# Hymba-style decoder block with PEER experts: both parts of the split weights kept in DRAM, and the raw U blocks moved to a pool of their own

## The chip, the cores and the metric

One core of a Trainium2 chip runs the whole layer in one launch. The metric is the device time of that core in microseconds (us), lower is better. The five compute engines are named as in the profile: PE (TensorE, with PEld for its weight loads), DVE (VectorE), ACT (ScalarE), POOL (GpSimd) and SP (SyncE, which here only issues DMAs).

## The reference

1024 tokens of width 1024 pass through one layer. What matters here is where the weight matrices are used:

```python
ada = jax.nn.silu(c) @ w_ada + b_ada          # shift, scale, gate of both norms
h = modulate(rms_norm(x, norm1_g), shift1, scale1)
proj = h @ w_in + b_in                        # q | k | v | B | C | u_conv, 2304 columns
mix = concat(head-normed attention, head-normed short gated conv) @ w_out + b_out
x = x + gate1 * mix
h2 = modulate(rms_norm(x, norm2_g), shift2, scale2)
q = h2 @ w_query                              # 8 heads x 256, 2048 columns
# PEER: top 16 of 16 x 16 pairs of keys per head, softmax gates,
#   a = gelu(h2 . peer_u[idx]);  y = sum(gate * a * peer_v[idx]),  16384 experts
x = x + gate2 * peer(h2, q);  return rms_norm(x, final_g)
```

## The kernel before

The tokens are eight tiles of 128. The **front** (everything up to the gates of PEER) runs in three groups: group 0 holds tiles 0, 1, 2, group 1 tiles 3, 4, 5 (both 384 tokens wide), group 2 tiles 6 and 7 (256 wide). After the front comes the **dense part**: for tiles 0, 1, 3, 4, 5 all 16384 experts are evaluated in blocks of 128 (U, then gelu, then the gates, then V), while for tiles 2, 6, 7 POOL gathers only the chosen rows of U and V by indirect DMA. The gathers and the making of the dense gates are spread beside the front and the dense part.

Every float32 matrix product is made of three matmuls in the rounded type fp32r. An operand X is split into H, X rounded, and L = X - H, and the product is H·h_H + H·h_L + L·h_H. `lin` (line 279) does this for one block of 128 output columns: 24 matmuls, for each of two halves of the rows first the eight that need H, then the four that need L.

The weights of the front are 42 such blocks in each group: 18 of w_in, 8 of w_out, 16 of w_query. One block is 512 KB of float32. The class `Weights` hands them out. `take()` gives the next block and calls `load()` for the one behind it, so that one block is prepared ahead of the one in use. `load()` does this:

- line 223: SP fetches the raw block into one of two buffers (tag `wraw`), in every group
- line 230: ACT makes H of each half (a copy with rounding), in every group
- line 232, group 0 only: POOL makes L of each half; line 225 writes L to a DRAM tile `low` at the next call, behind the next raw fetch
- line 235, groups 1 and 2: L comes back from `low` with a DMA of 256 KB a half

H and L have four buffers each (tags `wH`, `wL`), which is two blocks. In DRAM the rounded copy H is never kept, so ACT makes it anew in each group.

Other users of the same resources: `wada` (line 750), 48 blocks of 512 KB of w_ada, are fetched by SP in group 0 and reduced on DVE (`adaacc`, lines 754 and 756); the first 24 are needed before the first norm. `keyg` (line 631) brings the keys of a head in the query stage. In groups 1 and 2 the dense gates are made: `oh` (lines 834 to 847) on DVE, ACT and POOL, `G` (line 857) on PE, a copy to `stg` on ACT (line 858) and a DMA `G_d<-stg` (line 860) that ACT issues, 2 MB each in pieces of 256 bytes, 20 in all. The dense part begins with the fetch of two raw U blocks, the gates `Gb` and three V blocks; ACT makes UH (line 1096), POOL UL (line 1100), and PE starts with `A` (line 1133).

In the front a scheduler, which simulates the engines as the program is built, sets the order of the instructions of each engine; the dense part follows an order written out in the code. DMAs of SP and ACT take their completion semaphores in turn from a set of eight, and one that takes a semaphore waits until the DMA eight places before it has landed.

Of the kernel before, what the change touches and what calls it, by code (L numbers as in the profile page):

```python
# [9 lines left out]
F32 = mybir.dt.float32  # L10
F32R = mybir.dt.float32r
# [7 lines left out]
P = 128  # L19
# [3 lines left out]
NC = D // P  # L23
# [61 lines left out]
def block_kernel(  # L85
# [18 lines left out]
    nc = tc.nc  # L104
# [45 lines left out]
    gp = ctx.enter_context(tc.tile_pool(name="gp", bufs=ROWS[0]))  # L150
    gs = ctx.enter_context(tc.tile_pool(name="gs", bufs=1))
    slx = ExitStack()
    with ExitStack() as fctx:
# [48 lines left out]
        class Weights:  # L202


            def __init__(self):
                self.src = [(w_in, k) for k in range(18)] + [(w_out, k) for k in range(NC)]
                self.src += [(w_query, k) for k in range(16)]
                self.n = len(self.src)
                self.src *= len(GROUPS)
                self.at, self.ready = 0, []  # L210

                self.low = [dr.tile([P, 2, NC // 2, P], F32, name=f"low{k}") for k in range(self.n)]
                self.keep = []

            def load(self):
                if self.at == len(self.src):
                    return
                dram, k = self.src[self.at]
                name = f"{self.at}"
                low, first = self.low[self.at % self.n], self.at < self.n  # L220
                self.at += 1
                raw = fs.tile([P, NC, P], F32, tag="wraw", name=f"raw_{name}", bufs=2)
                nc.sync.dma_start(raw.rearrange("p c j -> p (c j)"), dram[k])
                while self.keep:
                    nc.sync.dma_start(*self.keep.pop(0))
                for q in range(2):
                    src = raw[:, q * (NC // 2) : (q + 1) * (NC // 2), :]
                    H = fs.tile([P, NC // 2, P], F32R, tag="wH", name=f"H_{name}_{q}", bufs=4)
                    L = fs.tile([P, NC // 2, P], F32R, tag="wL", name=f"L_{name}_{q}", bufs=4)
                    nc.scalar.copy(H, src)  # L230
                    if first:
                        nc.gpsimd.tensor_tensor(L, src, H.bitcast(F32), op=ALU.subtract)
                        self.keep.append((low[:, q], L.bitcast(F32)))
                    else:
                        nc.sync.dma_start(L.bitcast(F32), low[:, q])
                    self.ready.append((H, L))

# [774 lines left out]

        with tc.tile_pool(name="f0", bufs=1) as f0:
            rest = [lambda n=n: ada_rest(f0, n) for n in range(4, 12)]
            fronts[0].fp = f0
# [33 lines left out]
        gates_of = Beside(dense_gates(gg, [3, 4, 5]))  # L1049
        with tc.tile_pool(name="f2", bufs=1, reuse_waits="tile") as f2:  # L1050
            last.hH = f2.tile([P, NC, 2 * P], F32R, name="hSH")
            last.hL = f2.tile([P, NC, 2 * P], F32R, name="hSL")
# [20 lines left out]
    def dense_experts():  # L1073

        Up = {}
        Ur = {}
        Vr = {}
# [4 lines left out]
        def load_G(j):  # L1082

            if j < NK // GB:
                Gt[j] = dp.tile([P, NTG, GB * TG], F32, tag="G", name=f"Gb{j}", bufs=2)
                nc.sync.dma_start(Gt[j], G_d[j])

        def fetch_U(b):
            raw = dp.tile([P, NC, P], F32, tag="U", name=f"U{b}", bufs=2)
            nc.sync.dma_start(raw.rearrange("p c j -> p (c j)"), peer_uT[b])  # L1090
            Ur[b] = raw

# [112 lines left out]
        def load_ends():  # L1205

            gather.rest()
            for name, src in (("g2", g2_d[0]), ("fg", final_g)):
                r = dp.tile([P, NC, P], F32, tag="U", name=name, bufs=2).rearrange("p c j -> p (c j)")
                nc.sync.dma_start(r, src.partition_broadcast(P))  # L1210
                shared.append(r)
# [33 lines left out]

        fetch_U(0)
        fetch_U(1)
        for j in range(2):
# [160 lines left out]
```

## Time and profile before

| | |
|---|---|
| median of 3 runs | 2824.21 us (2823.27 to 2829.01) |
| profiled execution | 2822.61 us, span 2820.8 us, mean granted clock 0.974 |
| busy in the span | PE 2642.3 us (94%), DVE 2165.8 (77%), POOL 1696.2 (60%), ACT 1033.5 (37%) |
| group 0 of the front | 0 to 326 us, of which 0 to 46 before the first `lin` |
| group 1, group 2 | 326 to 664 us, 664 to 981 us |
| dense part | 981 to 2820 us |

The span is that of the engines' instructions; the execution's own time is 1.8 us longer, for what lies around them. The rows below come from the same execution. A row of busy times by stretch tells how full each engine and the DMA rings were there; the chain of waits tells which work ended last at each moment, and only what stands on that chain can shorten the run directly. The granted clock is TensorE's, 1.00 being 2.4 GHz.

### The profile page before, as it was taken

What the parts mean: (1) busy time and instruction counts of PE and PEld (TensorE: products, weight loads), DVE (VectorE), ACT (ScalarE), POOL (GpSimd) and SP (SyncE); (2) the same over time, 40 slices, a digit from 0 to 9 for tenths busy, and PEclk for the clock granted to TensorE, in tenths of its full rate; (3) what the DMA queues carried; (4) which work ended last, traced back from release to release, by engine and by line L of the source; (5) the groups of instructions that cost most, each with busy time, mean ns of one, the idle gap of its engine ahead of it and who ended that gap; (6) DMA issues with size and microseconds to landing.
All of it is one profiled execution on the core that took longest, in us unless ns stands there. A gap on an engine that the chain in (4) does not pass through costs nothing.

```text
span 2820.8 us, 44152 instructions
## 1 busy us (share of the span) xinstructions
PE 2642.3 (94%) x15358; PEld 2405.9 (85%) x15358; DVE 2165.8 (77%) x4645; ACT 1033.5 (37%) x2219; POOL 1696.2 (60%) x1726
## 2 busy tenths in 40 slices
PE   5998989988898869999999999999999999999997
PEld 4788977888788869999999899999998899999996
DVE  8835996879786877787777777777877777777776
ACT  3345555664667432222222222222222322222222
POOL 2334533523333247778777677777776777777771
PEclk9999999999999989999999999999999999999999
DMA  9757669986689949898889898989888888889884
GB/s 345 285 182 245 210 201 290 277 290 210 171 224 263 293 132 342 311 339 327 327 321 332 286 350 315 341 310 338 321 325 324 331 325 327 326 324 334 313 326 145
DMA packets 418268, 816.70 MB, mean 290 GB/s; under 512 B 192630, under 2 KB 198774, under 8 KB 418044
## 3 DMA queue, kind: packets, MB, share of 16 engines
q0 software_dynamic: 110592, 402.70, 38.8%
q1 hardware_dynamic: 143292, 369.24, 37.2%
q10 hardware_dynamic: 164160, 41.94, 6.9%
q8 instruction: 120, 1.97, 0.3%
q14 instruction: 104, 0.85, 0.1%
HBM read 739.83 MB, written 73.94 MB: 288 GB/s over the span
## 4 chain that ended last, share of the span: by engine, by line
PE 72%; DVE 13%; DMA 5%; issue 4%; ACT 3%; POOL 2%; SPq 0%; ACTq 0%; DVEq 0%; POOLq 0%
PE A L1133 29%; PE V L1179 29%; PE G L857 3%; PE lin_g1in L279 2%; DVE oh L834 2%; DVE adaacc L756 2%; DMA G_d<-stg 1%; PE lin_g0o L279 1%; DMA wada<-in_w_ada_dram 1%; PE lin_g2in L279 1%; PE po L430 1%; DVE Skg L143 1%; DVE ti L145 1%; PE lin_g2o L279 1%; DVE ti L142 1%
## 5 line engine op out<-in xcount | busy, mean ns | idle before, releaser
L960 POOL DMA_INDIRECT u<-in_peer_u_dram,idx x384 | 365.8, 952 | 264.5 <-DVE u L981 126.7
L1179 PE MATMUL V<-VH,WH 128*128 128x512 f32 x1280 | 501.4, 392 | 12.9 <-DVE acc_d L1186 10.3
L988 DVE SCALAR_TENSOR_TENSOR acc<-v,wv,acc 128x1024 f32<-128x1024 f32 x381 | 489.4, 1285 | 15.1 <-DMA v<-in_peer_v_dram,idx 10.9
L1179 PE MATMUL V<-VL,WH 128*128 128x512 f32 x1280 | 500.1, 391 | 0.0
L1179 PE MATMUL V<-VH,WL 128*128 128x512 f32 x1280 | 499.3, 390 | 0.0
L960 POOL DMA_INDIRECT v<-in_peer_v_dram,idx x384 | 363.5, 947 | 210.7 <-DVE u L981 69.1
L981 DVE SCALAR_TENSOR_TENSOR u<-u,h 128x1024 f32<-128x1024 f32 x384 | 457.7, 1214 | 5.8 <-DMA u<-in_peer_u_dram,idx 5.8
L1138 ACT ACTIVATE A<-A 128x384 f32<-128x384 f32 (+1 forms) x256 | 107.7, 422 | 955.7 <-PE A L1133 940.9
L1133 PE MATMUL A<-hDH,UH 128*128 128x384 f32 (+1 forms) x2048 | 345.5, 311 | 18.7 <-ACT UH L1096 18.1
L1116 POOL TENSOR_TENSOR VL<-V,VH 128x512 fp32r<-128x512 f32 x256 | 332.0, 1310 | 34.9 <-ACT VH L1112 32.6
L1133 PE MATMUL A<-hDH,UL 128*128 128x384 f32 (+1 forms) x2048 | 343.3, 310 | 8.5 <-POOL UL L1100 8.5
L1133 PEld LDWEIGHTS A<-hDH,UH 128*128 128x128 f32 x2048 | 321.9, 190 | 29.5 <-ACT UH L1096 18.9
L1133 PE MATMUL A<-hDL,UH 128*128 128x384 f32 (+1 forms) x2048 | 342.9, 310 | 0.0
L1100 POOL TENSOR_TENSOR UL<-U,UH 128x1024 fp32r<-128x1024 f32 x128 | 308.8, 2413 | 31.9 <-ACT UH L1096 29.7
L1133 PEld LDWEIGHTS A<-hDH,UL 128*128 128x128 f32 x2048 | 311.8, 189 | 9.8 <-POOL UL L1100 9.8
L1150 DVE TENSOR_TENSOR A<-A,Gb 128x384 f32<-128x384 f32 (+1 forms) x256 | 126.2, 498 | 248.3 <-ACT A L1138 243.6
L1133 PEld LDWEIGHTS A<-hDL,UH 128*128 128x128 f32 x2048 | 312.6, 190 | 0.0
L1179 PEld LDWEIGHTS V<-VH,WH 128*128 128x128 f32 x1280 | 241.3, 188 | 60.7 <-DVE acc_d L1186 12.0
L847 POOL TENSOR_TENSOR oh<-oh,gT 128x512 f32<-128x512 f32 x120 | 131.3, 1095 | 261.8 <-DVE oh L834 207.5
L1179 PEld LDWEIGHTS V<-VH,WL 128*128 128x128 f32 x1280 | 241.3, 188 | 51.4
L1179 PEld LDWEIGHTS V<-VL,WH 128*128 128x128 f32 x1280 | 241.3, 189 | 45.3
L1186 DVE TENSOR_TENSOR acc_d<-acc_d,V 128x512 f32<-128x512 f32 x310 | 211.7, 683 | 84.9 <-PE V L1179 84.8
(313 smaller groups left out, 4190.8 us busy)
## 6 DMA issues: line engine op xcount, KB each, us to landing
U<-in_peer_uT_dram SPq DMA_DIRECT2D x128, 512.0 KB, 7.7
V<-in_peer_v_dram SPq DMA_DIRECT2D x256, 256.0 KB, 3.8
L<-low SPq DMA_DIRECT2D x168, 256.0 KB, 4.0
G_d<-stg ACTq DMA_DIRECT2D x20, 2048.0 KB, 16.7
Gb<-G_d SPq DMA_DIRECT2D x64, 640.0 KB, 7.4
raw<-in_w_in_dram SPq DMA_DIRECT2D x54, 512.0 KB, 4.7
wada<-in_w_ada_dram SPq DMA_DIRECT2D x48, 512.0 KB, 6.8
raw<-in_w_query_dram SPq DMA_DIRECT2D x48, 512.0 KB, 5.2
```

Of the source, the lines that this page charges most:

```text
L279: nc.tensor.matmul(ps[:, :w], wt[:, c, :], h[:, q * (NC // 2) + c, o : o + w], start=(k == 0), stop=(k == 3 * NC - 1),)
L847: nc.gpsimd.tensor_tensor(og, og, gT[:, t0 : t0 + 4].unsqueeze(2).to_broadcast([P, 4, NK]), op=ALU.mult)
L960: nc.gpsimd.indirect_dma_start(out=t, out_offset=None, in_=peer_u if which == "u" else peer_v, in_offset=bass.IndirectOffsetOnAxis(ap=idx[ ...
L981: nc.vector.scalar_tensor_tensor(t, t, 1.0, h2[i], op0=ALU.mult, op1=ALU.mult, accum_out=av[i][:, j : j + 1])
L988: nc.vector.scalar_tensor_tensor(acc[i], t, wv[i][:, j : j + 1], acc[i], op0=ALU.mult, op1=ALU.add)
L1100: nc.gpsimd.tensor_tensor(L, Ur.pop(b), Up[b][0].bitcast(F32), op=ALU.subtract)
L1116: nc.gpsimd.tensor_tensor(L, Vr.pop(v), Vp[v][0].bitcast(F32), op=ALU.subtract)
L1133: nc.tensor.matmul(ps[:, : n * P], u[:, c, :], h[:, c, sl], start=(k == 0), stop=(k == 3 * NC - 1))
L1138: nc.scalar.activation(w, w, AF.Gelu)
L1150: nc.vector.tensor_tensor(w3, w3, g, op=ALU.mult)
L1179: nc.tensor.matmul(ps, w[:, ts_], v, start=(n == 0), stop=(n == 3 * CB - 1))
L1186: nc.vector.tensor_tensor(accs[0][:, t, hs], accs[0][:, t, hs], ps, op=ALU.add)
```

## The change

1. In place of `low` (L alone) the DRAM tile `kept` holds H and L of a half side by side. Group 0 writes one tile `HL` of 512 KB a half where it wrote 256 KB. Groups 1 and 2 fetch `HL` with one DMA of 512 KB a half; they fetch no raw block and make no H on ACT.
2. The buffers of H and L become one tag `wHL` with four buffers, of the same size in all. The two raw buffers exist only in the pool `f0`, which is freed after group 0.
3. A new pool `up`, opened ahead of the front, holds the raw U blocks (two buffers); the pool `dp` of the dense part has none any more. The fetch of U blocks 0 and 1 is written at the head of the last group's block instead of at the head of the dense part. The last loads of the kernel (`g2`, `fg`) use `up` too.

```diff
+    up = ctx.enter_context(tc.tile_pool(name="up", bufs=1, reuse_waits="tile"))
+    Ur = {}
+
+    def fetch_U(b):
+        raw = up.tile([P, NC, P], F32, tag="U", name=f"U{b}", bufs=2)
+        nc.sync.dma_start(raw.rearrange("p c j -> p (c j)"), peer_uT[b])
+        Ur[b] = raw
...
-                self.low = [dr.tile([P, 2, NC // 2, P], F32, name=f"low{k}") for k in range(self.n)]
+                self.kept = [dr.tile([P, 2, 2, NC // 2, P], F32, name=f"kept{k}") for k in range(self.n)]
...
-                raw = fs.tile([P, NC, P], F32, tag="wraw", name=f"raw_{name}", bufs=2)
-                nc.sync.dma_start(raw.rearrange("p c j -> p (c j)"), dram[k])
+                if first:
+                    raw = self.raw.tile([P, NC, P], F32, tag="wraw", name=f"raw_{name}", bufs=2)
+                    nc.sync.dma_start(raw.rearrange("p c j -> p (c j)"), dram[k])
                 while self.keep:
                     nc.sync.dma_start(*self.keep.pop(0))
                 for q in range(2):
-                    src = raw[:, q * (NC // 2) : (q + 1) * (NC // 2), :]
-                    H = fs.tile([P, NC // 2, P], F32R, tag="wH", name=f"H_{name}_{q}", bufs=4)
-                    L = fs.tile([P, NC // 2, P], F32R, tag="wL", name=f"L_{name}_{q}", bufs=4)
-                    nc.scalar.copy(H, src)
+                    HL = fs.tile([P, 2, NC // 2, P], F32R, tag="wHL", name=f"HL_{name}_{q}", bufs=4)
+                    H, L = HL[:, 0], HL[:, 1]
                     if first:
+                        src = raw[:, q * (NC // 2) : (q + 1) * (NC // 2), :]
+                        nc.scalar.copy(H, src)
                         nc.gpsimd.tensor_tensor(L, src, H.bitcast(F32), op=ALU.subtract)
-                        self.keep.append((low[:, q], L.bitcast(F32)))
+                        self.keep.append((kept[:, q], HL.bitcast(F32)))
                     else:
-                        nc.sync.dma_start(L.bitcast(F32), low[:, q])
+                        nc.sync.dma_start(HL.bitcast(F32), kept[:, q])
...
         with tc.tile_pool(name="f0", bufs=1) as f0:
+            weights.raw = f0
...
         with tc.tile_pool(name="f2", bufs=1, reuse_waits="tile") as f2:
+            for b in range(2):
+                fetch_U(b)
...
-        fetch_U(0)
-        fetch_U(1)
         for j in range(2):
             load_G(j)
```

The line numbers of the changed program are 8 or 9 higher in the front than before. Three places show what the scheduler makes of it.

SP, near the program's start, before the first norm. `wada` are the blocks of w_ada, `low` the DRAM tile of L, `raw` a weight block. First the program before:

```order
L750 DMA wada_0_277<-in_w_ada_dram 128x1024
L631 DMA keyg_1_2207<-in_keysT_dram 128x128
L750 DMA wada_1_281<-in_w_ada_dram 128x1024
L750 DMA wada_2_285<-in_w_ada_dram 128x1024
L750 DMA wada_3_289<-in_w_ada_dram 128x1024
L750 DMA wada_0_300<-in_w_ada_dram 128x1024
L225 DMA low_166<-L_0_391 128x512
L225 DMA low_166<-L_1_395 128x512
L223 DMA raw_459<-in_w_in_dram 128x1024
L750 DMA wada_1_304<-in_w_ada_dram 128x1024
```

And the same place in the changed program:

```order
L759 DMA wada_0_280<-in_w_ada_dram 128x1024
L640 DMA keyg_1_2154<-in_keysT_dram 128x128
L157 DMA U_7021<-in_peer_uT_dram 128x1024
L759 DMA wada_1_284<-in_w_ada_dram 128x1024
L157 DMA U_7023<-in_peer_uT_dram 128x1024
L759 DMA wada_2_288<-in_w_ada_dram 128x1024
L759 DMA wada_3_292<-in_w_ada_dram 128x1024
L759 DMA wada_0_303<-in_w_ada_dram 128x1024
L234 DMA kept_169<-HL_0_393 128x1024
L234 DMA kept_169<-HL_1_396 128x1024
L232 DMA raw_458<-in_w_in_dram 128x1024
L759 DMA wada_1_307<-in_w_ada_dram 128x1024
```

The two fetches of U stand here, among the first `wada`, and not with the last group: their buffers are free from the start, and nothing holds them back. The writes behind the second block of `wada` are twice as wide.

SP, in the last third of group 2's query stage, ahead of the dense part. Before, a block is four DMAs (raw, two L, a key):

```order
L223 DMA raw_10799<-in_w_query_dram 128x1024
L235 DMA L_1_10670<-low_204 128x512
L235 DMA L_0_10742<-low_205 128x512
L235 DMA L_1_10746<-low_205 128x512
L631 DMA keyg_12_10735<-in_keysT_dram 128x128
L223 DMA raw_10875<-in_w_query_dram 128x1024
L235 DMA L_0_10802<-low_206 128x512
L631 DMA keyg_13_10795<-in_keysT_dram 128x128
L235 DMA L_1_10806<-low_206 128x512
```

In the changed program it is three:

```order
L244 DMA HL_0_10106<-kept_207 128x1024
L640 DMA keyg_11_10102<-in_keysT_dram 128x128
L244 DMA HL_1_10108<-kept_207 128x1024
L244 DMA HL_0_10176<-kept_208 128x1024
L244 DMA HL_1_10178<-kept_208 128x1024
L640 DMA keyg_12_10172<-in_keysT_dram 128x128
L244 DMA HL_0_10230<-kept_209 128x1024
L640 DMA keyg_13_10226<-in_keysT_dram 128x128
L244 DMA HL_1_10232<-kept_209 128x1024
```

The raw fetches are gone, and each remaining fetch of weights is 512 KB instead of 256. The order among the blocks is the same.

ACT, at the same place, behind the last but one write of gates. `qqsg` is a block of queries, `Skg` the scores of a head. Before:

```order
L860 DMA G_d<-stg_3_10067 128x64x64
L230 CAST H_0_10665<-raw_10663 128x512
L650 COPY Skg_9_10519<-pkg_9_0_10563 128x256
L230 CAST H_1_10669<-raw_10663 128x512
L640 COPY qqsg_10_10601<-lin_g2q_0_10613 128x256
L230 CAST H_0_10741<-raw_10739 128x512
L230 CAST H_1_10745<-raw_10739 128x512
L650 COPY Skg_10_10602<-pkg_10_0_10639 128x256
L640 COPY qqsg_11_10661<-lin_g2q_0_10673 128x256
```

In the changed program:

```order
L869 DMA G_d<-stg_3_9552 128x64x64
L659 COPY Skg_9_9974<-pkg_9_0_10012 128x256
L649 COPY qqsg_10_10050<-lin_g2q_0_10056 128x256
L659 COPY Skg_10_10051<-pkg_10_0_10082 128x256
L649 COPY qqsg_11_10104<-lin_g2q_0_10110 128x256
```

The copies of H no longer stand between the other copies of ACT, here and in all of groups 1 and 2 (168 of them).

## Rows read from the trace of the kernel before

**Rows 1.** The page's first part: busy time of each engine in the span.

```profile
PE 2642.3 (94%) x15358; PEld 2405.9 (85%) x15358; DVE 2165.8 (77%) x4645; ACT 1033.5 (37%) x2219; POOL 1696.2 (60%) x1726
```

**Rows 2.** Busy time by stretch, with granted clock, DMA share and GB/s.

```profile
core 0: us, PE busy (x) PEld busy (x) DVE busy (x) ACT busy (x) POOL busy (x), PEclk, DMA share, GB/s
20.00:40.00 20.00, 3.73 (x16) 3.56 (x16) 17.41 (x22) 4.25 (x6) 6.01 (x4) 1.00 1.03 408
40.00:60.00 20.00, 18.33 (x99) 18.14 (x100) 19.77 (x35) 9.03 (x17) 4.79 (x3) 1.00 0.83 301
60.00:80.00 20.00, 18.82 (x111) 18.05 (x111) 19.68 (x23) 6.59 (x12) 11.32 (x8) 1.00 1.02 379
80.00:100.00 20.00, 19.80 (x110) 15.96 (x108) 14.50 (x39) 8.77 (x26) 5.24 (x4) 0.91 0.90 346
326.00:985.00 659.00, 583.36 (x3903) 534.64 (x3903) 530.50 (x1758) 376.72 (x887) 221.89 (x380) 0.95 0.81 244
497.00:577.00 80.00, 69.04 (x463) 65.59 (x463) 60.91 (x82) 55.30 (x146) 38.80 (x38) 0.95 0.93 288
1061.00:1550.00 489.00, 489.00 (x2756) 446.73 (x2755) 382.88 (x539) 135.83 (x263) 375.83 (x318) 1.00 0.90 329
```

**Rows 3.** The chain of waits from 0 to 47 us: start, length, what.

```profile
13.36 9.58 DMA wada<-in_w_ada_dram
...
30.93 7.47 DMA wada<-in_w_ada_dram
```

**Rows 4.** Line 225, the writes of L in group 0, from 55 to 95 us.

```profile
L225 SPq DMA_DIRECT2D low<-L x12: 326/380/1356, 55.1 to 90.4; - x12
...
DMA to landing us min/median/max: 5.4/6.1/7.0
```

**Rows 5.** The page's DMA issues: engine, count, KB each, median us to landing.

```profile
L<-low SPq DMA_DIRECT2D x168, 256.0 KB, 4.0
...
G_d<-stg ACTq DMA_DIRECT2D x20, 2048.0 KB, 16.7
...
raw<-in_w_query_dram SPq DMA_DIRECT2D x48, 512.0 KB, 5.2
```

**Rows 6.** Line 230 from 326 to 985 us: ns min/median/max, first and last start.

```profile
L230 ACT CAST H<-raw x164: 602/620/639, 329.4 to 972.6; 128x512 fp32r<-128x512 f32 x164
```

**Rows 7.** The chain of waits in groups 1 and 2.

```profile
335.62 0.62 ACT H L230
336.77 15.01 PE lin_g1in L279 x85
...
938.35 4.24 DMA raw<-in_w_query_dram
...
944.49 5.88 DMA raw<-in_w_query_dram
...
950.92 0.61 ACT H L230
...
977.48 3.03 PE lin_g2q L279 x24
```

**Rows 8.** Waits from 326 to 985 us: engine, line, waited for, total, times, longest.

```profile
ACT H L230 <- PE lin_g1in L279: 31.6, 27, 2.1
...
PE oTg L590 <- ACT osg L585: 7.0, 6, 2.7
PE lin_g2q L279 <- DMA L<-low: 6.8, 3, 5.7
```

**Rows 9.** Waits of SP's DMA queue from 326 to 985 us.

```profile
SPq L235 <- DMA G_d<-stg: 30.5, 4, 8.9
...
SPq L223 <- DMA G_d<-stg: 23.8, 4, 8.4
```

**Rows 10.** Timeline at the start of the dense part.

```profile
982.76 2.00 ACT L1096 CAST UH<-U 128x1024 fp32r<-128x1024 f32 x2
...
987.58 4.76 POOL L1100 TENSOR_TENSOR UL<-U,UH 128x1024 fp32r<-128x1024 f32 x2
```

More of the change, by code (lines that the diff above doesn't have):

```diff
@@ L219, in load @@
                 name = f"{self.at}"
-                low, first = self.low[self.at % self.n], self.at < self.n
+                kept, first = self.kept[self.at % self.n], self.at < self.n
                 self.at += 1
-                raw = fs.tile([P, NC, P], F32, tag="wraw", name=f"raw_{name}", bufs=2)
-                nc.sync.dma_start(raw.rearrange("p c j -> p (c j)"), dram[k])
+                if first:
+                    raw = self.raw.tile([P, NC, P], F32, tag="wraw", name=f"raw_{name}", bufs=2)
+                    nc.sync.dma_start(raw.rearrange("p c j -> p (c j)"), dram[k])
                 while self.keep:
@@ L1075, in dense_experts @@
         Up = {}
-        Ur = {}
         Vr = {}
@@ L1086, in load_G @@
                 nc.sync.dma_start(Gt[j], G_d[j])
[L1088 to L1091, printed above, removed]
         def split_U(b, part):
@@ L1208, in load_ends @@
             for name, src in (("g2", g2_d[0]), ("fg", final_g)):
-                r = dp.tile([P, NC, P], F32, tag="U", name=name, bufs=2).rearrange("p c j -> p (c j)")
+                r = up.tile([P, NC, P], F32, tag="U", name=name, bufs=2).rearrange("p c j -> p (c j)")
                 nc.sync.dma_start(r, src.partition_broadcast(P))
```

## The prediction

> **What bounds the kernel now.** I read the busy times first, then the busy times by stretch, then the chain of waits, and only then single waits. PE is busy for 2642.3 us of the span, no other engine for more than 77% of it [rows 1]. The stretches say where that leaves room. From 1061 us on PE is busy in every one of 489.00 us at clock 1.00 [rows 2]: two thirds of the run are TensorE's alone, and the change leaves that order of work as it is. So its worth lies ahead of 1061 us. In groups 1 and 2 PE is busy 583.36 of 659 us [rows 2], so 75.6 us is all that could be won there without touching its work. At the other end stands the program's start: from 20 to 40 us PE works 3.73 us while the DMA rings are full (share 1.03, 408 GB/s) [rows 2], and the chain there passes through two fetches of w_ada of 9.58 and 7.47 us [rows 3]. The reader should see two different kernels in one: a start that waits for bytes, and groups 1 and 2 which wait for many small things, ACT among them.
>
> **What the change costs at the start.** The order on SP shows that the two raw U blocks are not fetched with the last group: they stand among the first eight fetches of w_ada. That is 2 x 512 KB = 1.05 MB ahead of bytes that the chain waits for. The four writes of the first two weight blocks also stand there, each now 512 KB instead of 256: another 1.05 MB. At 408 GB/s [rows 2] 2.1 MB take 5.1 us. The second fetch on the chain lands at 38.4 us [rows 3], behind all of them. The least is 0, if DVE's reductions between the two fetches, 22.9 to 30.9 us, take it up; the most is 5.1. The rings are full, so I take the value that full rings give: **+5**.
>
> **The rest of group 0.** From 55 to 95 us there are 12 writes of L [rows 4]. They grow by 12 x 262 KB = 3.1 MB, which is 7.7 us at 408 GB/s. Rings that are 1.02 full from 60 to 80 us leave nothing; 0.83 and 0.90 on either side leave 3.4 and 2.0 us [rows 2]. PE is busy 18.3, 18.8 and 19.8 of 20 us in these three stretches, so some of a late block shows at once and some is worked off beside it. A second wait is new: a buffer of H could be filled again when its matmuls were done, and now also only when its write has landed, which took 6.1 us in the full stretch [rows 4]. ACT takes its work in order, so later copies queue behind such an H. Behind 95 us the rings have room for the other writes. Ends 0 and 7.7 (the bytes at full price); I take **+2**, nearer the low end, since PE is nearly full there in any case.
>
> The Trainium skill ("DMA: Bandwidth & Descriptors", Anatomy of one DMA) speaks against this part: it puts most of a transfer's fixed cost into the receipt of the last write, and calls DRAM the heaviest target. By it a write holds its buffer for longer than a read of equal size takes. The trace doesn't show that: where the rings are full a write of 256 KB landed in 6.1 us [rows 4], less than the 7.47 us in which 512 KB of w_ada were read [rows 3]. The sum would go to the upper end of this term by the page, +7.7.
>
> **What it saves in groups 1 and 2: ACT.** The 168 copies of H leave, 620 ns each [rows 6], 104 us of the 376.7 us that ACT is busy there [rows 2]. Most of it stood beside PE's work. On the chain the copies appear in ten pieces, the first of 0.62 us at 335.62 and the last of 0.61 at 950.92 [rows 7], 6.7 us in sum. But a copy also stands still on ACT when its buffer isn't free: 27 times for `lin_g1in` alone, 31.6 us [rows 8], with ACT's other work queued behind it. PE waits for such work, for instance 7.0 us for `osg` [rows 8]. So the low end is 2 us (a third of the chain's pieces, if DVE, the next in line in most of them, is as late), the high end 6.7 + 7.0 + half the 31.6 = 29; I take the chain's share and a little for the queueing: **-8**.
>
> **Raw fetches and the rings' semaphores.** Two raw fetches stood on the chain at 938 and 944 us, 4.24 and 5.88 us [rows 7]. They go, but HL must now be fetched at that place; ends 0 and -10, I take **-3**. SP also stands for `G_d<-stg` eight times at 30.5 + 23.8 us [rows 9]: such a write takes 16.7 us [rows 5], and the DMA eight places behind it waits for its semaphore, with all fetches queued behind that one. With three DMAs a block in the query stage instead of four (two instead of three elsewhere), the eighth is for a block further on: SP comes to it one block later, 3 to 4 us [rows 7]. Half of the stall goes. PE saw little of it, 6.8 us in three waits for L [rows 8], so the ends are 0 and -7, and I take **-3**.
>
> **What it costs there: later landings.** A half of L (256 KB) landed after 4.0 us, a block of 512 KB after 5.2 [rows 5]. HL is a transfer of the second kind, and its first matmul needs it eight matmuls earlier than L was needed. The cover is four half-buffers: a buffer comes free half-way through a block and is needed one and a half blocks later. In group 1, 85 matmuls take 15.01 us [rows 7], so 36 take 6.4 us: 5.2 is hidden. In group 2, 24 take 3.03 us, so 36 take 4.5 us [rows 7]: back to back blocks fall 0.7 us behind each. Most are not back to back: 42 blocks in 319 us are one in 7.6 us. If the 16 blocks of the query stage were, it would be 11 us; if none, nothing. I take four or five blocks, **+3**. Bytes don't change there: 512 + 2 x 256 before, 2 x 512 now, so the rings, at 0.81 over both groups and 0.93 from 497 to 577 us [rows 2], are as full as they were.
>
> The Trainium skill (same page and section) fits a DMA as about 2.0 us fixed and the bytes at 436 GB/s, an estimate of 3.2 us for 512 KB and 2.6 for 256. By that nothing falls behind in group 2 and the term is 0. The trace's rows have 1.2 us between the two sizes where the page has 0.6, beside other traffic, and they decide here.
>
> **The dense part's start.** UH begins at 982.76 us, without a wait for U, and POOL takes UL at 987.58, when its own earlier work is done [rows 10]. U that has long landed wins nothing by itself; what goes is 1.05 MB ahead of the first V, 2.6 us at 408 GB/s, and V's copies stand behind the same ACT and POOL work. Ends 0 and -3, I take **-0.5**. Two issues of U leave SP's queue there and stand at the start, under 1 us each way, beside transfers that take longer.
>
> **The sum:** 5 + 2 - 8 - 3 - 3 + 3 - 0.5 = -4.5 us. From the profiled execution's 2822.6 us that is 2818.1. That execution is 1.6 us below the median of the runs, so I forecast 2820 us for the median.
>
> **The rivals.**
> *Faster by more.* The start absorbs its bytes behind DVE (+1), group 0 hides its writes (0), ACT gives -10, the raw fetches -5, the semaphores -4, HL lands in time (0), the dense start gives 0: -18 us, about 2806. For it: ACT's queue delays several kinds of work, and 31.6 us of standing copies in one stage is much [rows 8]. Against it: from 326 to 985 us DVE is busy 530.5 of 659 us [rows 2], so it soon is the next that's late.
> *Slower: the rings in group 0.* One mechanism, bytes ahead of w_ada and of the raw blocks: the start pays 5.1 us, and the full stretch from 60 us pays its 7.7 us, while H waits for its own write. If ACT's relief is worth no more than 2 us and HL's later landing costs what the raw fetches and semaphores give back, the sum is 5 + 8 + 0 = +13 us after -2 for ACT and +2 for the blocks that wait on H, about 2837. It decides where the rings stay at 1.0 until the last `wada` is in, and no stretch with spare follows before PE needs it. For it: 1.03 and 1.02 [rows 2]. Against it: the 20 us from 40 have 0.83. The page's rule on the receipt of a write, named above, would push this way too; the rows have no sign of it so far.
> *The change doesn't do what it says.* For U this is sure, by the order, and is in the sum: its 1.05 MB cost about 2.6 us at the start in place of a place in the last group. It has no chance of its own.
>
> **How the numbers follow.** About 0.2%, 5.6 us, is what a measurement of this kernel can tell from no change. Forecast: 0.40, with its own range from -10 to +3 us, so 0.16 of faster and 0.24 within the bound. Faster by more: 0.30, of it 0.28 faster and 0.02 within. Slower: 0.26, of it 0.24 slower. The last 0.04, an order of the scheduler with a new stall that I don't see, goes half to each side. Faster 0.46, same 0.27, slower 0.27, with 0.01 of the forecast counted as slower. The range must reach both rivals' times: 2804 to 2837 us.
>
> **What would show it.** Right at the start: the first `lin` of group 0 about 5 us later, and the two U among the first DMAs. Group 0 ends at about 333 us instead of 326. In groups 1 and 2 ACT is busy some 273 us instead of 376.7, no line of H on the chain, SP's waits for `G_d<-stg` about halved, HL landing in about 5 us; group 2's last `lin` comes some 4 us earlier than at 980.5. The dense part has the same length within 1 us. Wrong would be: group 0 longer by over 10 us (then the rings were the bound), or `lin` waiting for HL for over 10 us in group 2 (then the fetch ahead is too short), or groups 1 and 2 shorter by 20 us and more (then ACT's queue was worth more than its place on the chain).

## The result: slower by 1.1%

The changed kernel takes 2854.43 us (median of 4 runs, 2852.95 to 2863.21) against 2825.39 us: a ratio of 1.0109, 95% interval 1.0088 to 1.0131. The forecast was 2820 us, its range ended at 2837. The profiled execution took 2863.21 us, span 2861.4. The page's first part and the busy times by stretch of the changed kernel, with the columns of [rows 1, 2]; the stretch from 341 to 1021 us is groups 1 and 2:

```profile
PE 2658.5 (93%) x15358; PEld 2425.1 (85%) x15358; DVE 2160.0 (75%) x4645; ACT 941.5 (33%) x2051; POOL 1690.2 (59%) x1726
```

```profile
20.00:40.00 20.00, 3.73 (x16) 3.56 (x16) 15.26 (x19) 4.33 (x7) 6.01 (x4) 1.00 1.03 404
60.00:80.00 20.00, 18.83 (x109) 17.71 (x108) 19.38 (x23) 5.19 (x10) 8.20 (x6) 1.00 0.88 313
80.00:100.00 20.00, 15.35 (x87) 13.86 (x87) 12.06 (x35) 7.49 (x23) 5.48 (x4) 0.83 1.03 417
341.00:1021.00 680.00, 594.62 (x3893) 545.12 (x3893) 531.24 (x1731) 284.26 (x718) 222.69 (x381) 0.92 0.79 237
1100.00:1589.00 489.00, 489.00 (x2760) 446.86 (x2760) 381.85 (x537) 135.41 (x263) 374.82 (x318) 1.00 0.90 330
```

From 1100 us on the dense part is what it was. Groups 1 and 2 ended at 980.5 us before, and the row of [rows 2] runs 4.5 us on into the dense part. This row of the kernel before ends closer to them:

```profile
326.00:982.00 656.00, 581.77 (x3896) 533.24 (x3896) 527.50 (x1737) 374.45 (x884) 221.40 (x378) 0.95 0.81 243
```

ACT works 90 us less in groups 1 and 2, and still they are some 25 us longer. The two rows show two halves of that. PE stands 85.4 us there instead of 74.2 (the length of the stretch less the time PE is busy), and it is busy 594.6 instead of 581.8 us with the same matmuls, at a granted clock of 0.92 instead of 0.95.

What PE waits for in this stretch (engine, line, waited for, total, times, longest):

```profile
PE lin_g2q L288 <- DMA HL<-kept: 17.5, 5, 8.1
...
PE hssg L461 <- ACT sqg L459: 4.8, 1, 4.8
PE lin_g1q L288 <- DMA HL<-kept: 4.0, 1, 4.0
PE lin_g2in L288 <- DMA HL<-kept: 3.8, 3, 2.0
PE oTg L599 <- ACT osg L594: 3.6, 3, 2.2
```

Where [rows 8] had 6.8 us for L, 25.3 us now go to HL. The wait for ACT's `osg` fell from 7.0 to 3.6 us, but that for its `sqg` rose from 0.8 to 4.8. All waits of PE for ACT in groups 1 and 2 sum to 33.3 us before and 31.9 us now, so hardly any of ACT's relief reaches PE.

SP's stands behind the writes of gates, in the same stretch:

```profile
SPq L640 <- DMA G_d<-stg: 22.1, 2, 12.2
...
SPq L244 <- DMA G_d<-stg: 8.5, 1, 8.5
SPq L361 <- DMA G_d<-stg: 6.3, 1, 6.3
```

They are four, 36.9 us in all. Before there were ten of 71.3 us, the eight of [rows 9] and these two:

```profile
SPq L610 <- DMA G_d<-stg: 9.3, 1, 9.3
...
SPq L623 <- DMA G_d<-stg: 7.7, 1, 7.7
```

So they are fewer, as forecast, but the longest is 12.2 us, where it was 9.3. How such a stand reaches PE, the chain of waits shows from 948 us on (start, length, what):

```profile
949.00 20.22 DMA G_d<-stg
...
969.29 0.33 SPq L640
...
969.73 4.84 DMA HL<-kept
...
974.62 2.93 PE lin_g2q L288 x12
```

ACT issues a write of gates at 949.00. It lands at 969.2. SP has meanwhile issued seven DMAs (timeline of SP):

```profile
950.51 0.32 SPq L632 DMA_DIRECT2D h2d<-xng  x1
950.93 2.08 SPq L244 DMA_DIRECT2D HL<-kept  x2
953.10 1.40 SPq L640 DMA_DIRECT2D keyg<-in_keysT_dram  x1
954.58 1.10 SPq L632 DMA_DIRECT2D h2d<-xng  x1
955.77 1.26 SPq L244 DMA_DIRECT2D HL<-kept  x2
969.29 0.33 SPq L640 DMA_DIRECT2D keyg<-in_keysT_dram  x1
969.73 0.85 SPq L244 DMA_DIRECT2D HL<-kept  x2
```

The eighth is a small fetch of keys. SP stands 12 us for it, and HL of the next block, whose buffers are free, queues behind. PE runs out of weights at 969 us and stands 5.66 us. Of PE's ten waits for HL, three end this way behind a stand of SP, those of 4.0, 5.7 and 8.1 us: 17.7 of 25.6 us. The granted clock is low there too:

```profile
955.00:965.00 10.00, 7.75 (x53) 7.56 (x53) 10.00 (x56) 2.86 (x8) 4.28 (x12) 0.83 1.06 347
965.00:975.00 10.00, 4.34 (x36) 4.14 (x35) 8.17 (x54) 1.33 (x3) 3.07 (x11) 0.82 0.73 183
975.00:985.00 10.00, 10.00 (x75) 10.00 (x75) 6.19 (x35) 2.57 (x6) 2.87 (x11) 0.84 0.75 252
985.00:995.00 10.00, 10.00 (x87) 9.95 (x85) 7.73 (x58) 2.67 (x6) 2.32 (x12) 1.00 0.92 262
```

From 975 to 985 us PE is busy all the time, but at 0.84: part of it at the lower level, 1.2 GHz, behind the stand. So 75 matmuls fit where ten us later 87 do.

The table gives the length of each part, read from the starts and ends of PE's instructions in each trace, in us. "Start" ends with the first `lin`; group 0 ends with group 1's first `lin`, groups 1 and 2 with group 2's last `lin`. The waits are PE's for the kept weights (before: for L and H).

| kernel | start | group 0 | groups 1, 2 | dense part | waits for weights | median, ratio |
|---|---|---|---|---|---|---|
| before | 46.5 | 280.0 | 654.1 | 1840.3 | 9.9 | 2825.4 |
| the change | 52.4 | 288.8 | 679.7 | 1840.5 | 25.6 | 2854.4, 1.0109 |
| after_again | 52.1 | 282.2 | 676.9 | 1846.7 | 25.7 | 2859.7, one run |
| after_b | 51.9 | 287.0 | 674.0 | 1848.2 | 24.0 | 2861.5, 1.0109 |
| e1_u_late | 49.4 | 278.7 | 681.5 | 1839.6 | 23.7 | 2860.2, 1.0122 |
| e1_b | 49.3 | 279.1 | 679.7 | 1846.6 | 20.4 | 2864.2, 1.0120 |
| f2_kept_rows | 49.4 | 281.6 | 658.2 | 1844.8 | 12.4 | 2846.1, 1.0075 |
| e8_bufs5 | 49.5 | 280.6 | 655.4 | 1853.8 | 7.0 | 2842.7, 1.0045 |
| e5_bufs6 | 49.3 | 281.3 | 651.3 | 1839.8 | 0 | 2837.0, 1.0040 |
| e5_b | 49.6 | 282.2 | 654.8 | 1841.3 | 0.3 | 2835.9, 1.0040 |

Each ratio is to the kernel before on the same chips; that one had medians from 2823.8 to 2828.8 us. A part's length is that of the one profiled execution and the median that of all runs, so the parts of two kernels can differ by more or less than their medians do.

### The profile page after: what moved, and what is told of

The parts are those of the page before. It is cut to its first block, busy times and chain, and to the rows that moved or that the text cites. A ratio compares the mean times of both kernels' runs of the same rounds, so it can differ in the third digit from the quotient of the medians.

```text
span 2861.4 us, 43778 instructions
## 1 busy us (share of the span) xinstructions
PE 2658.5 (93%) x15358; PEld 2425.1 (85%) x15358; DVE 2160.0 (75%) x4645; ACT 941.5 (33%) x2051; POOL 1690.2 (59%) x1726
## 4 chain that ended last, share of the span: by engine, by line
PE 75%; DVE 12%; DMA 6%; issue 2%; ACT 2%; POOL 2%; SPq 0%; ACTq 0%; DVEq 0%; POOLq 0%
PE A L1139 29%; PE V L1185 29%; PE G L866 3%; DMA G_d<-stg 2%; PE lin_g0in L288 2%; PE lin_g1q L288 2%; DVE oh L843 2%; PE lin_g2in L288 1%; DMA wada<-in_w_ada_dram 1%; DVE adaacc L765 1%; PE po L439 1%; PE lin_g2q L288 1%; DMA HL<-kept 1%; PE lin_g1in L288 1%; PE lin_g1o L288 1%
## 5 line engine op out<-in xcount | busy, mean ns | idle before, releaser
L1185 PE MATMUL V<-VH,WH 128*128 128x512 f32 x1280 | 502.6, 393 | 13.2 <-DVE acc_d L1192 11.2
```

Of the source, the lines that this page charges most:

```text
L1185: nc.tensor.matmul(ps, w[:, ts_], v, start=(n == 0), stop=(n == 3 * CB - 1))
```

## The experiments

### The parts of the change, one at a time

**e1_u_late** takes the pool `up` out again; U is in `dp` and fetched at the dense part's start, as before:

```diff
-    up = ctx.enter_context(tc.tile_pool(name="up", bufs=1, reuse_waits="tile"))
-            for b in range(2):
-                fetch_U(b)
+            raw = dp.tile([P, NC, P], F32, tag="U", name=f"U{b}", bufs=2)
+        fetch_U(0)
+        fetch_U(1)
```

> The change without its part on U: the raw U blocks are in the dense part's pool and are fetched at its start, as before; both weight parts are kept as in the change. Theory: the two U blocks among the first fetches of w_ada delay the first lin by about 2.6 us (1.05 MB at 408 GB/s), so without them the first lin starts near 49.5 us (46.5 before, 52.4 with the change), and the run takes 2848 to 2851 us. Rival, U is hidden behind other fetches and the order alone moved: first lin at 52 us, the run within 3 us of the change's 2854.

Measured: the first `lin` at 49.4 us, as the theory says, 3.0 us earlier than with the change. But the run takes 2860.2 us (1.0122, 1.0106 to 1.0137), more than theory and rival gave.

**e1_b** and **after_b** are that kernel and the changed one again, side by side on one chip.

> e1_u_late once more, beside the changed kernel on one chip, for the price of the early U. Theory, U early costs the 3 us by which the first lin is later, and up to 10 us at the end of w_in in group 0, of which less than half is left at the end: 2848 to 2858 us, 0 to 8 us under after_b. Rival, U early costs nothing or wins at the start of the dense part: within 3 us of after_b or above it.

> The changed kernel beside e1_b on the same chip: 2852 to 2862 us. Its profile is the third of this kernel: w_in's lin of group 0 end at 196 to 200 us as in the two before, 15 us later than in the kernels with U late and wide writes (180 to 185).

Measured: 2864.2 us (1.0120, 1.0102 to 1.0138) and 2861.5 us (1.0109, 1.0089 to 1.0128). The early U costs nothing that the whole run can tell. At the front it does: start plus group 0 are 334 to 341 us in three profiles of the change and 328 in the two without early U. A part of these 6 to 13 us is in the traces. In w_in's `lin` of group 0 PE waits 4.8 to 6.0 us for copies of H in the three, 1.7 and 2.7 in the two and 0.5 before, most of it behind a raw block that took 10.1 to 11.1 us to land (chain of the changed kernel):

```profile
72.10 11.14 DMA raw<-in_w_in_dram
...
83.31 0.63 ACT HL L240
...
83.98 5.94 PE lin_g0in L288 x24
```

Without early U a raw block at this place took 8.2 us (e1_u_late). In groups 1 and 2 the three profiles get 0 to 7 us back. Why the medians show nothing of the rest is open.

**after_again**, the changed kernel for a second profile:

> The changed kernel itself once more, for a second profile. If the first profile is typical: w_in's lin of group 0 end near 200 us (174.3 before), group 0 ends near 339, group 2 near 1021, and PE waits for HL about 25 us in groups 1 and 2. If its group 0 was an unlucky execution, w_in's lin end near 185 us as in e5_bufs6 and e1_u_late, and the run takes about 2853 us.

Measured: 2859.7 us; w_in of group 0 ends at 196 us, group 2 at 1011, PE waits 25.7 us for the kept weights. The waits repeat; group 0 ends 7 us sooner than in the first profile, at 334 us, and group 2 10 us sooner.

**e2_wide** is the kernel before with group 0 writing both parts, for which H and L share a buffer:

```diff
-                    H = fs.tile([P, NC // 2, P], F32R, tag="wH", ..., bufs=4)
-                    L = fs.tile([P, NC // 2, P], F32R, tag="wL", ..., bufs=4)
+                    HL = fs.tile([P, 2, NC // 2, P], F32R, tag="wHL", ..., bufs=4)
+                    H, L = HL[:, 0], HL[:, 1]
-                        self.keep.append((low[:, q], L.bitcast(F32)))
+                        self.keep.append((low[:, q], HL.bitcast(F32)))
-                        nc.sync.dma_start(L.bitcast(F32), low[:, q])
+                        nc.sync.dma_start(L.bitcast(F32), low[:, q, 1])
```

> The kernel before with one thing of the change: group 0 writes H and L, 512 KB a half; groups 1 and 2 still fetch the raw block, make H on ACT and fetch L alone. Theory: the wider writes on full DMA rings are what lengthens group 0, so w_in's lin of group 0 end about 15 to 20 us later than before's 174.3 us, groups 1 and 2 keep their length, and the run takes 2837 to 2845 us. Rival, the loss in group 0 comes from something else in the change (raw buffers in another pool, U, another order): within 5 us of 2825.

Measured: 2847.4 us (1.0076, 1.0060 to 1.0092), above the theory's range, and its place was wrong: start 49.5, group 0 280.6 us. The first `lin` is 3.0 us later, group 0 as long as before, and groups 1 and 2 took 671 us.

**p3_joint** is e2_wide with the narrow writes: one buffer for H and L, and nothing else.

> The kernel before with H and L of a half in one buffer (tag wHL, four of them, the same bytes in all) and nothing else: group 0 writes L alone, groups 1 and 2 fetch the raw block, make H on ACT and fetch L. Not a byte more or less is moved than before; what is new is that a copy of H waits for L's use and L's write too, and that the scheduler finds another order. Theory, what e2_wide lost behind group 0 (13 us) comes from the shared buffer and the order, not from wider writes: 2834 to 2842 us, with group 0 as before (within 3 us). Rival, the wider writes did it: within 4 us of before's 2826.

Measured: 2839.9 us (1.0046, 1.0028 to 1.0064), start and group 0 no longer than before, groups 1 and 2 667 us. So a shared buffer, with the order that comes with it, cost 13 us without a byte more. Its row of groups 1 and 2:

```profile
321.00:989.00 668.00, 593.75 (x3893) 547.23 (x3891) 528.12 (x1732) 370.70 (x882) 223.29 (x377) 0.93 0.79 238
```

PE stands 74.2 us in it, no longer than before. The loss is in the time that PE is busy, at 0.93. Against p3_joint the wider writes of e2_wide cost 8 us by the ratios: 3.0 us of its profile at the start, 5.9 in group 0 and 3.8 in groups 1 and 2.

**e3_narrow** is e1_u_late with narrow writes; groups 1 and 2 fetch 512 KB a half:

```diff
-                        self.keep.append((kept[:, q], HL.bitcast(F32)))
+                        self.keep.append((kept[:, q], L.bitcast(F32)))
-                        nc.sync.dma_start(HL.bitcast(F32), kept[:, q])
+                        nc.sync.dma_start(HL.bitcast(F32), kept)
```

> The other half: U late, group 0 writes L alone (256 KB a half), and groups 1 and 2 fetch 512 KB a half with no raw block and no copy on ACT. Those 512 KB are the L of both halves, so H is left out of what groups 1 and 2 read. Theory: the fetch of HL in groups 1 and 2 costs more than ACT's relief gives, PE waits for HL some 25 us there, group 0 ends where it did before (326 us), and the run takes 2837 to 2846 us. Rival, groups 1 and 2 only pass on group 0's delay and are no longer by themselves: 2825 us or less, 2815 to 2828.

Measured: 2843.6 us (1.0058, 1.0043 to 1.0072), as the theory said: group 1 starts at 323 us, and groups 1 and 2 take 679 us by themselves, with 19.7 us of waits for weights. So their loss needs no wider writes. But e1_u_late, with the wider writes, takes 16.6 us more by the medians, and its profiled execution only 4.6 us more. What the wider writes cost in all lies between 3 us (the start, in every profile) and these 17; both pairs of kernels may differ in order too.

### How far ahead HL is fetched

**e5_bufs6**, **e5_b** and **e8_bufs5** are e1_u_late with `bufs=6` (twice) and `bufs=5` in place of `bufs=4` of `wHL`.

> As e1_u_late, with six half-buffers for HL instead of four (three blocks instead of two). Theory: four half-buffers are too few ahead, so PE's waits for HL in groups 1 and 2 fall from 25 us to under 8, and the run is 10 to 18 us shorter than e1_u_late. Rival, SP's queue and the writes of the gates make HL late whatever the buffers: within 4 us of e1_u_late.

> e1_u_late with five half-buffers for HL, between its four (2860 us) and the six of e5_bufs6 (2837 us). Theory, the short cover costs these 23 us: PE waits for HL between 20.6 and 0 us in groups 1 and 2, and the run takes 2842 to 2853 us. Rival, e5_bufs6 won by its order: 2856 us or more, or as fast as with six, 2838 us or less.

> e5_bufs6 once more, for a second profile (its first profiled execution, 2823 us, was the fastest of its runs, the median 2837). If six half-buffers really end the waits for HL, PE waits for HL under 3 us in groups 1 and 2, and these two groups take 648 to 660 us together (677 to 682 with four, 654 before); the run takes 2832 to 2842 us. If the first profile was luck, the groups take 665 us or more.

Measured: 2837.0 (1.0040, 1.0026 to 1.0053), 2835.9 (1.0040, 1.0025 to 1.0055) and 2842.7 us (1.0045, 1.0030 to 1.0059). Groups 1 and 2 follow the number: 680 to 682 us with four, 655 with five, 651 and 655 with six. The waits of PE for HL in e1_b, e8_bufs5 and e5_b, in that order:

```profile
PE lin_g2q L280 <- DMA HL<-kept: 14.9, 4, 5.9
PE lin_g1q L280 <- DMA HL<-kept: 3.4, 1, 3.4
```

```profile
PE lin_g2q L280 <- DMA HL<-kept: 6.2, 4, 3.5
```

```profile
PE lin_g2in L280 <- DMA HL<-kept: 0.3, 1, 0.3
```

And the stands of SP in e5_b, beside its busy times in groups 1 and 2:

```profile
SPq L236 <- DMA G_d<-stg: 47.9, 6, 11.5
SPq L632 <- DMA G_d<-stg: 18.3, 2, 12.4
```

```profile
331.00:987.00 656.00, 582.86 (x3892) 534.97 (x3891) 525.27 (x1722) 284.27 (x718) 219.01 (x371) 0.95 0.80 242
```

SP stands longer than in the change, 66 us, and the weights are in time all the same: three blocks of cover outlast the stand. The keys, though, come late:

```profile
PE pkg L644 <- DMA keyg<-in_keysT_dram: 7.4, 3, 5.9
```

Before, PE waited 3.1 us for keys; the 5.9 us come behind the stand of 12.4 us. PE is busy 582.9 us, the clock is at 0.95 again. The kernel without waits for HL is as long in groups 1 and 2 as the kernel before, not shorter. PE's waits for ACT there sum to 33.0 and 34.5 us in e5_bufs6 and e5_b, and to 33.3 in the kernel before: 90 us of ACT's work taken away gave PE nothing. e5_bufs6 is 23 us shorter than e1_u_late, more than the theory's 10 to 18. In e8_bufs5 the dense part of the profiled execution is 12 to 14 us longer than with six, and why isn't shown.

**f2_kept_rows** and **f1_before_rows** make the writes of gates short, in e1_u_late and in the kernel before:

```diff
-                                G_d.rearrange("b p g f -> p g b f")[:, tg0 + tg],
-                                stg.rearrange("p (b e) t -> p b (e t)", e=GB),
+                                G_d.rearrange("b p g f -> (b p g f)").rearrange("(t p x) -> t p x", t=NTG, p=P)[tg0 + tg],
+                                stg.rearrange("p b t -> p (b t)"),
```

> The kernel before, with the 20 writes of gates going to G_d in rows of 16 KB a partition instead of pieces of 256 bytes. The gates land in another order in G_d than the dense part reads them in, so its sums are over the wrong gates; amount of data and all other work are the same. A write should land in 5 to 8 us instead of 16.7. Theory, SP's stands behind these writes and their place on the chain cost the kernel before little (PE waits 6.8 us for L): 2812 to 2822 us. Rival, they cost nothing that the rest doesn't take back: 2822 to 2828 us.

> e1_u_late with the same writes of gates in rows of 16 KB (sums over the wrong gates, the same work). Theory, the long writes of gates are what makes HL late: SP doesn't stand for them any more (under 10 us in all in groups 1 and 2, 37 in e1_u_late), PE waits for HL under 8 us (20.6 in e1_u_late), and the run is 18 to 30 us shorter than e1_u_late's 2860, so 2830 to 2842 us; what is left over f1_before_rows is the wider writes in group 0, 5 to 10 us, and it takes more off this kernel than off the kernel before. Rival, HL is late by itself (512 KB in four half-buffers): PE still waits 15 us and more, and the run is shortened by no more than f1_before_rows is, under 8 us.

Measured: 2824.5 us (0.9992, 0.9980 to 1.0005) and 2846.1 us (1.0075, 1.0055 to 1.0094). In the kernel before they cost nothing, the rival. In the changed one they do: 14 us less than e1_u_late, and groups 1 and 2 at 658 us. SP stands 2.7 us behind them in place of 35, PE waits 12.4 us for HL instead of 20 to 24:

```profile
PE lin_g2q L280 <- DMA HL<-kept: 7.3, 4, 4.3
```

The 12.4 us that are left lie above the theory's 8 and below the rival's 15, and the run is 4 us above the theory's range: about half of the waits for HL are the writes', and part of the late HL isn't.

**e6_split** gives H and L their own buffers (four each) and DMAs of 256 KB; **e7_whole3** has one buffer and one DMA of 1 MB for a block, three of them:

```diff
+                        nc.sync.dma_start(H.bitcast(F32), kept[:, q, 0])
+                        nc.sync.dma_start(L.bitcast(F32), kept[:, q, 1])
...
+                W = fs.tile([P, 2, 2, NC // 2, P], F32R, tag="wHL", name=f"HL_{name}", bufs=3)
+                    nc.sync.dma_start(W.bitcast(F32), kept)
```

> As e1_u_late (U late, H and L both kept, no raw block and no copy on ACT in groups 1 and 2), but H and L in buffers of their own, each written and fetched by a DMA of 256 KB. Theory, SP's queue is what makes HL late: with four to five DMAs a block in place of two to three, SP comes to the DMA eight places behind a write of gates sooner and stands longer (over 90 us for these writes in groups 1 and 2, 37 in e1_u_late), so PE waits for H and L as long as in e1_u_late or longer and the run takes 2855 to 2875 us. Rival, the 512 KB transfer is what lands too late (5.1 us median against 4.0): PE's waits for the kept weights fall below 8 us and the run takes 2835 to 2848 us.

> As e5_bufs6 (the same 48 KB of buffers for three blocks), but one buffer holds a whole block and one DMA of 1 MB fetches or writes it. Theory, SP's stand behind the writes of gates: one or two DMAs a block put the eighth four and more blocks behind such a write, SP stands for them less than 25 us in groups 1 and 2 (66 in e5_bufs6), PE waits for HL under 8 us, and the run takes 2826 to 2838 us, no longer than e5_bufs6. Rival, a whole block comes later into a buffer that is freed later (cover of two blocks instead of two and a half, landing of some 8 us): PE waits for HL over 15 us and the run takes 2845 us or more.

Measured: 2852.7 us (1.0093, 1.0068 to 1.0117) and 2831.8 us (1.0020, 1.0004 to 1.0037). In e6_split SP stands 90 us and PE waits 17.8 us for the kept weights, so smaller transfers don't help, though the run is just under what the theory gave. In e7_whole3 SP stands 36 us, more than the theory's 25, but PE waits 1.8 us for HL, and it is the fastest kernel that keeps H. It doesn't beat the kernel before, and no kernel here does.

### What another order is worth

**p4_rawpools** has the raw buffers in each group's pool, **g1_L5** five buffers for L and **g2_H5** five for H in the kernel before:

```diff
+                raw = self.raw.tile([P, NC, P], F32, tag="wraw", name=f"raw_{name}", bufs=2)
...
+                    L = fs.tile([P, NC // 2, P], F32R, tag="wL", name=f"L_{name}_{q}", bufs=5)
...
+                    H = fs.tile([P, NC // 2, P], F32R, tag="wH", name=f"H_{name}_{q}", bufs=5)
```

> The kernel before with the raw weight buffers in the pool of each group (f0, f1, f2) instead of the pool of the whole front: the same work, the same bytes, the same number and size of buffers; the scheduler finds another order (some 200 of PE's 6046 instructions stand elsewhere). It asks what another order alone is worth. Theory, the order of the kernel before is a lucky one and any other costs about what p3_joint lost: 2832 to 2842 us. Rival, the order is worth little and p3_joint lost by its shared buffer: within 4 us of 2825.

> The kernel before with five buffers for halves of L instead of four, in room that was free. If the cover of two blocks is what limits the kernel before as well, PE's waits for L in group 2's query stage (6.8 us) go and the run takes 2812 to 2821 us; if two blocks are enough as long as raw blocks are fetched two further ahead, it stays within 4 us of 2825.

> The kernel before with five buffers for halves of H instead of four, in room that was free: no other work and no other bytes, one more buffer, another order (180 places on PE). g1_L5, which differs from it in the same small way, took 21 us more than before. Theory, that was an accident of its order, and orders of this kernel lie between 2822 and 2850 us: anything in there, more likely 2824 to 2840. Rival, a fifth buffer does harm by itself (fetches that come earlier push others back): 2845 us or more again.

Measured: 2825.5 us (1.0004, 0.9993 to 1.0015), 2850.3 us (1.0076, 1.0058 to 1.0095) and 2825.7 us (1.0004, 0.9991 to 1.0017). Another order costs nothing in two of the three, and in f1_before_rows, a third. In g1_L5 it costs 21 us: group 1 is 355 us long instead of 340, with 1.6 us of waits for weights in it. g2_H5, with one buffer more as well, loses nothing, which speaks for the order; whether it is the order or the fifth buffer of L wasn't separated, and which place does harm was not found. So a loss of 10 or 20 us in one kernel with a new order may be the order's. The loss that goes with the number of half-buffers shows in eight profiles: 674 to 682 us of groups 1 and 2 in the five with four half-buffers, 651 to 655 in the three with five and six. An accident of one order is not a likely cause of that. Nor does a wait for weights always lengthen the run: p4_rawpools has 23.5 us of waits for L and H in its profile, and its groups 1 and 2 are 656 us long, since PE waits less for other things there.

## Why the prediction was wrong

**The start** held: +5 was forecast, the first `lin` came 5.9 us later. The runs split it: 3.0 us for the wider writes (e2_wide), 2.5 to 3.0 for U, about the 2.6 us for its 1.05 MB that 408 GB/s give [rows 2]. The chain goes through `wada` as before, and more of it is waiting for them (chain of the changed kernel, beside [rows 3]):

```profile
13.45 9.59 DMA wada<-in_w_ada_dram
...
25.20 8.71 DMA wada<-in_w_ada_dram
...
33.98 10.36 DMA wada<-in_w_ada_dram
```

Before, DVE's reductions stood on the chain between a landing at 22.9 and a fetch at 30.93. Now two fetches follow each other from 25.20 on, and the reductions there are hidden behind the transfers.

**The rest of group 0**, +2 with ends 0 and 7.7: with U late it is 279 to 282 us in all kernels with wide writes, against 280. With U early it is 282 to 289. The end that was named is reached and passed in the first profile, but only where U is early. From the span's start, group 0 ends 8, 12 and 15 us later in the three profiles (7 forecast), which is the size that the rival "the rings in group 0" gave this part; the sign that was named for it, over 10 us, came in two of them. That the full rings did it isn't shown: from 80 to 100 us they are as full, at 1.03, in the two kernels without early U. The second wait, H behind its own write, shows once in each, 2.5 or 2.6 us of ACT. The writes, now twice as large, landed after 8.8 us in the full stretch instead of 6.1 [rows 4].

The rows don't bear out the Trainium skill's rule on the receipt of a write ("DMA: Bandwidth & Descriptors", Anatomy of one DMA), which that section gives for DMAs issued by POOL, while these are SP's. From 80 to 100 us of the changed kernel, with the rings at 1.03, the writes of 512 KB landed after 8.6 us (median), reads of equal size after 8.7 (raw) and 8.9 (w_ada). The profile's DMA issues of the whole run, where the reads of HL stand in groups 1 and 2 and the writes in group 0:

```profile
HL<-kept SPq DMA_DIRECT2D x168, 512.0 KB, 5.1
...
kept<-HL SPq DMA_DIRECT2D x84, 512.0 KB, 4.2
```

**ACT**, -8: this failed. 90 us of its work left where 104 were forecast (284.3 us of work against "some 273"), but e5_bufs6 and e5_b show what that gives when HL is in time: groups 1 and 2 at 651 and 655 us, before 654. Neither the copies on the chain nor the copies that stood on ACT were worth time to PE, whose waits for ACT stayed at 32 to 35 us. The rival's objection, that another engine is the next that is late, fits that; which work took the place of the chain's 6.7 us wasn't traced.

**The raw fetches**, -3: they left the chain, but HL took their place there, as the end of 0 said, and more. The fetch at 969.73 is one of its pieces, and in all HL's fetches are 3.8% of the chain from 341 to 1021 us, some 26 us.

**The semaphores**, -3: the size of SP's stand was right (71 us in ten stands before, 37 in four now, "about halved"), the conclusion wrong. A stand counts by its length against the cover, not by its share. SP was to come to the eighth DMA 3 to 4 us later. At the last two writes of gates it came 10.3 and 7.0 us behind the write before, and 8.0 and 9.1 us now, since small transfers take their turns too. The writes themselves took longer, 20.2 and 19.0 us instead of 18.0 and 15.3. So the two stands grew from 7.7 and 8.3 to 12.2 and 9.9 us.

**The later landings**, +3: this is the step that failed most, and it is where the time went. The cover was reckoned right, 36 matmuls, 4.5 us in group 2. It was held against the median landing, 5.2 us, and the median is not what hurts: 5.1 us was measured, and most blocks were in time. What hurts is a landing behind SP's stand, 12.2 us and then 4.8 for the transfer. The prediction had the landing and the stands of the kernel before, up to 8.9 us [rows 9], in two paragraphs, and did not add them; 8.9 us alone are twice the cover. PE waited 25 us for HL, and its matmuls took some 13 us more at a lower granted clock. Groups 1 and 2 came out 20 to 26 us longer in the three profiles, where -11 (ACT, raw, semaphores and HL together) was forecast. The runs tie this to the stands and the cover: with five and six half-buffers the waits are 7 us and nothing and the length is back, and with short writes of gates (f2_kept_rows) it is 4 us from that of the kernel before. What part of it comes with the shared buffer alone isn't separated: p3_joint lost 13 us in the same groups with nothing else of the change, but e6_split, with buffers of their own, lost 17, and the kernels with five and six half-buffers, shared as well, lost 1 us at most. That the halves of L had been fetched no further ahead than HL is now made the two look alike; but L was half the size and needed eight matmuls later. The sign that it named, over 10 us of waits for HL in group 2, came in, with 21 us.

**The dense part**, -0.5: within 1 us in the first profile, 6 and 8 us longer in the other two. e1_b, with U fetched late as before, has the same 6, so this isn't the early U's; nothing shows a gain from it.

**The sum** of the first profile: 5.9 us at the start, 8.8 in group 0, 25.6 in groups 1 and 2, 0.2 in the dense part, 40.5 us together. The medians are 29 us apart: this execution was the slowest of the changed kernel's four, and that of the kernel before lay 3 us under its median. e5_b, without waits for HL and without early U, is still 10.6 us above the kernel before when timed. Its profile shows 6.9 of them: 3 us at the start, 2 in group 0 and 1 or less in each of the other parts. The rest is open.

## What to carry to other kernels

How far ahead a buffer set fetches must be held against the longest time for which the queue in front of it can stand, not against the median landing: two half-buffers more took 23 us back here. Work taken from an engine that the chain hardly touches can be worth nothing, whatever its busy time: 90 us of ACT were. And what a scheduler may move it can move far: here a fetch into a buffer that is free from the start went to the start, though it was written with the last group.

## What the runs showed of the hardware

The time that PE stands isn't all that a change can cost it. In groups 1 and 2 PE stood 11.2 us longer with the change, and its matmuls took another 12.8 us, at a granted clock of 0.92 instead of 0.95; in e5_b, without waits for HL, both came back. But the clock doesn't follow the length of the stands: PE of p3_joint stood 74.2 us, as before, and that of f1_before_rows 63.5 us, and they were busy 593 and 595 us, at 0.93. What made the clock lower there is open. One kernel's executions spread by 7 to 21 us here, and the first profile of e5_bufs6, at 2823 us, was its fastest: a median of several runs, and a second profile, were needed to read differences of this size.
